# Two trunk layers on one core: index queries for 384 tokens, bias tables in tiles of their own, first x tiles on two queues

## The chip, the cores and the metric

The kernel runs on one core of one Trainium2 chip. The metric is device time in microseconds (us) of one execution, given as the median of three runs. A profiled execution has its own time; the span inside it runs from the first to the last instruction.

## What is computed

Two layers follow one another on 512 tokens of width 2048, in float32. Layer 0 (even) norms x, projects it and feeds two branches; the change is in the branch that picks keys:

```python
h = rms_norm(x, norm_g) @ w_in
p_in, p_gate, dq, dk, dv, d_gate, iq, ik, iw = split_cols(h, EVEN_SPLITS)
...
# per block of 128 queries, starting at token `start`:
s_idx = einsum('bqhe,bse->bqhs', iqb, ik) * IDX_DIM ** -0.5     # 16 index heads of 64
score = einsum('bqhs,bqh->bqs', relu(s_idx), iwb)
score = where(keys <= pos_q, score, -inf)
_, idx = top_k(score, 128)                                      # topk = 512 // 4
# attention over the chosen keys, with a T5 bias table
```

A query among the first 128 tokens has at most 128 keys, so the choice keeps all of them; the kernel computes index scores for the query blocks 1, 2 and 3 alone. Layer 1 (odd) is a sliding window attention with the same kind of bias table, and both layers end in an output projection and a residual sum.

## The kernel before

**Products.** Each float32 operand is held as two parts, a rounded one and the rest. One product of a 128x128 weight block is three matmuls, the helper `mm3` (lines 127 to 129). A projection is a job of 16 steps over the 2048 input channels in blocks of 128 (`col_job`): its step k multiplies weight block k by `acts[k]`, the transposed and split x of that block, with 512 tokens as moving columns. Jobs wait in a queue, and `pump(n)` emits n steps of it. `later(n, f)` calls f after n more steps.

**Weights.** `load_to` issues the loads of weight tiles `wr` on SyncE's (SP's) DMA queue; `split_to` has ScalarE (ACT) write the rounded part `wh` (line 101) and VectorE (DVE) the rest `wl` (line 107).

**The start.** Ahead of all jobs stands a loop over k = 0 to 15 that has its matmuls written out. Below, "tile k" is x's channel block k. `x_tile(k)` turns tile k by four transposes on TensorE (PE) into a PSUM bank of tag O (line 640), from which ACT writes the rounded part scaled by the norm gain (line 642), DVE the rest (line 643), and ACT (even k) or DVE (odd k) a copy (line 646) that SP stores to DRAM (line 647). Tag O has two banks, handed out in turn, and whoever takes a bank waits until its last content has been read. Step k of the loop holds: `mm3` on the first block of index queries, `x_tile(k + 2)`, the splits of coming weights, and twelve matmuls of 256 columns for keys, values and index keys (line 703, "the small group" below). Beside that ACT squares two pieces of x per step in the steps 3 to 10 (line 718). All engines work through their instructions in the order in which the program emits them.

**The first loads.** SP issues tile 0, two weight tiles, tile 1, then the first 512 channels of x (tiles 2 and 3 are read from these), a third weight tile and the next 512 channels. ACT issues the three gain vectors.

**Bias tables.** `bias_rows` (line 655) loads a one-hot table into a tile of tag `s2` (four buffers, which the copies of line 646 use too), emits a product with the bias table three steps later on PE, into a bank of tag O (line 661), and one step later a copy by ACT (line 665) and a store. It is called in steps 8, 9 and 10.

**After the loop** come seven jobs, of 16 steps each, for the other blocks of index queries. Among their steps stand `spread` (line 350, two banks of tag O), the key transposes and the index scores (line 974: 256, 384 and 512 columns). Then the choice of keys and all later work follow.

Of the kernel before, what the change touches and what calls it, by code (L numbers as in the profile page):

```python
# [10 lines left out]
F32 = mybir.dt.float32  # L11
# [3 lines left out]
OP = mybir.AluOpType  # L15
# [20 lines left out]
def trunk(ctx, tc, x, rel_bias, even_norm, even_w_in, even_pool_w, even_pool_scale, even_q_gain,  # L36
# [14 lines left out]
    def s2k():  # L51
        return sb.tile([P, 512], F32, tag="s2", name="s2", bufs=4)
# [73 lines left out]
    def mm3(o, wh, wl, xh, xl, start, stop):  # L126
        PE.matmul(o, wh, xh, start=start, stop=False)  # L127
        PE.matmul(o, wh, xl, start=False, stop=False)  # L128
        PE.matmul(o, wl, xh, start=False, stop=stop)  # L129
# [4 lines left out]

    def col_job(acts, w, ncols, c0, finish, hook=None):

        us = [plan_cols(w, ncols, c0, k0) for k0 in (0, 8)]

        def run():
            acc = bank("acc")  # L140
            for k in range(NK):
                u = us[k // 8] + k % 8 // 4
                hi, lo = view(u, 4)
                a = acts[k]
                flush(("split", id(a)))
                mm3(acc, hi[:, k % 4, :], lo[:, k % 4, :], a[:, 0, :], a[:, 1, :], k == 0, k == NK - 1)
                if k % 4 == 0:
                    split_to(u + 1 + AHEAD)
                if hook:
                    hook(k)  # L150
                if k == NK - 1:
                    finish(acc)
                yield
        queue.append(run())
        count["queued"] += NK
# [86 lines left out]

    def load_first(k):
        x_first[k] = s2k()
        nc.sync.dma_start(out=x_first[k].rearrange("p (i c) -> p i c", i=NT),
                          in_=ap(x2, k * P, [[D, P], [P * D, NT], [1, P]]))

    load_first(0)
    load_to(2)
    load_first(1)  # L250
    load_x(0)
    load_to(3)
    load_x(1)

# [8 lines left out]
    gain0, gain1, pscale = vecs[:, 0:16], vecs[:, 16:32], vecs[:, 32:40]  # L263
    vrow = sb.tile([P, 512], F32, tag="gt", name="vrow", bufs=2)[0:40, 0:P]
    qg0 = cst.tile([P, 1], F32, name="qg0")
# [4 lines left out]
    relb = cst.tile([33, 32], F32, name="relb")  # L270
    for r0, n, src in ((0, NK, even_norm), (16, NK, odd_norm), (32, 8, even_pool_scale)):
        nc.scalar.dma_start(out=vrow[r0:r0 + n], in_=ap(src, 0, [[P, n], [1, P]]))
# [381 lines left out]
    def bias_rows(oh, n0, n1, heads, dst):  # L654
        n = n1 - n0
        t = s2k()
        nc.sync.dma_start(out=t[0:33, :n], in_=oh[:, n0:n1])
# [22 lines left out]
    for j in range(1, 8):  # L680
        col_job(acts, w_in0, E_IN, IQ + j * P, lambda acc: stack(acc, P, 384, then=iq_st.append))
    split_to(1)
    vb = bank("O")
    PE.transpose(vb[:, 0:40], vrow, ident[0:40, 0:40])
    V.tensor_copy(out=vecs, in_=vb[:, 0:40])
    V.tensor_scalar(out=pscale, in0=pscale, scalar1=2.0, scalar2=None, op0=OP.mult)
    x_tile(0)
# [4 lines left out]
    for k in range(NK):  # L692
        sh, sl = view(s_half[k], 2)
        ih, il = view(q_half[k], 4)
        a = acts[k]
        mm3(iq_ps[0], ih[:, k % 4, :], il[:, k % 4, :], a[:, 0, :], a[:, 1, :], k == 0, k == NK - 1)
        if k + 2 < NK:
# [8 lines left out]
        if k == 1:  # L706
            load_x(2)
        if k == 3:
            load_x(3)
        if k == 6:  # L710
            load_constants()
        if k in (8, 9, 10):
            bias_rows(*((onehot0, 0, 512, 16, rv0), (onehot0, 512, 640, 16, rv0),
                        (onehot1, 0, 512, 32, rv1))[k - 8])
        if 3 <= k < 11:
# [187 lines left out]
    split_to(done["split"] + 4)  # L903
    stack(iq_ps[0], P, 384, then=iq_st.append)
    ssk = cst.tile([P, NT], F32, name="ssk")
# [323 lines left out]
```

## Time and profile before

| what | us |
|---|---|
| median of three runs | 1434.77 (1432.28 to 1435.99) |
| the profiled execution | 1435.47 |
| its span, first to last instruction | 1433.7 |
| TensorE busy in the span | 1414.7 |
| VectorE busy | 886.0 |
| ScalarE busy | 735.9 |

A row of the trace's timeline gives the start of an instruction or of a run of equal ones, its duration, its engine and line, what it writes and reads, and in brackets how long the engine had been idle and what released it. Matmuls overlap, so the rate of a stretch is read from the starts of its rows and not from their durations.

### The profile page before, as it was taken

To read this page: it belongs to the slowest core of one execution; us is meant where nothing else is said; L and a number is where in the kernel's file an instruction comes from. 1 tells how busy PE (TensorE), PEld (TensorE's weight loads), DVE (VectorE), ACT (ScalarE), POOL (GpSimd) and SP (SyncE) were. 2 spreads that over 40 slices of the span, in tenths; PEclk is the share of its full clock that TensorE was granted. 3 is DMA by queue.
4 is the path that set the end of the run, shared out by engine and by line. 5 is a ranking of instruction groups with operands and counts; after the bars stand their busy time and mean duration, and the time that the engine had idled before them with its cause. 6 is when DMAs were issued, how large, how long until landed. Compare 5 with 4: busy or idle time off the path is not lost.

```text
span 1433.7 us, 19902 instructions
## 1 busy us (share of the span) xinstructions
PE 1414.7 (99%) x7149; PEld 1180.3 (82%) x7149; DVE 886.0 (62%) x1663; ACT 735.9 (51%) x1641; POOL 331.7 (23%) x469
## 2 busy tenths in 40 slices
PE   7999999999999999999999999999999999999998
PEld 6788888888888888788888888788888888888887
DVE  4555679845687777733335468777777777753332
ACT  6544422323567676633335357666776757742221
POOL 1100001324546553111111143232232323100000
PEclk9999999999999999999999999999999999999999
DMA  9432333333432322265543232233232322334442
GB/s 286 139 88 74 89 103 89 96 102 96 114 82 86 103 74 74 74 173 144 147 139 103 86 113 85 71 96 100 80 101 85 96 86 84 100 118 154 129 158 74
DMA packets 228439, 153.84 MB, mean 107 GB/s; under 512 B 9001, under 2 KB 205698, under 8 KB 228340
## 3 DMA queue, kind: packets, MB, share of 16 engines
q1 hardware_dynamic: 228260, 152.55, 36.1%
q8 instruction: 56, 0.92, 0.3%
q14 instruction: 43, 0.35, 0.1%
q10 hardware_dynamic: 80, 0.02, 0.0%
HBM read 139.85 MB, written 12.69 MB: 106 GB/s over the span
## 4 chain that ended last, share of the span: by engine, by line
PE 91%; ACT 2%; DMA 2%; DVE 2%; issue 1%; SPq 1%; POOL 1%; DVEq 0%; ACTq 0%; POOLq 0%
PE ps_acc L127 21%; PE ps_acc L128 21%; PE ps_acc L129 21%; PE ps_S L171 5%; PE ps_T L171 5%; PE ps_O L523 3%; PE ps_S L459 3%; PE ps_acc L171 3%; PE ps_O L171 3%; PE ps_T L498 3%; PE ps_S L974 1%; DMA wr<-in_even_w_in 1%; DMA G<-rv 1%; DVE wl L107 1%; PE ps_O L855 0%
## 5 line engine op out<-in xcount | busy, mean ns | idle before, releaser
L107 DVE TENSOR_TENSOR wl<-wr,wh 128x512 fp32r<-128x512 f32 x440 | 332.7, 768 | 169.1 <-ACT wh L101 167.3
L101 ACT CAST wh<-wr 128x512 fp32r<-128x512 f32 x440 | 265.7, 617 | 225.6 <-PE ps_acc L128 89.0
L127 PE MATMUL ps_acc<-h,wh 128*128 128x512 f32 x640 | 254.5, 398 | 0.0
L128 PE MATMUL ps_acc<-h,wh 128*128 128x512 f32 x640 | 250.1, 391 | 0.0
L129 PE MATMUL ps_acc<-h,wl 128*128 128x512 f32 x640 | 250.1, 391 | 0.0
L127 PE MATMUL ps_acc<-h1s,wh 128*128 128x512 f32 x512 | 207.3, 405 | 0.0
L128 PE MATMUL ps_acc<-h1s,wh 128*128 128x512 f32 x512 | 200.7, 392 | 0.0
L129 PE MATMUL ps_acc<-h1s,wl 128*128 128x512 f32 x512 | 200.6, 392 | 0.0
L129 PEld LDWEIGHTS ps_acc<-h,wl 128*128 128x128 f32 x640 | 120.3, 188 | 26.4
L127 PEld LDWEIGHTS ps_acc<-h,wh 128*128 128x128 f32 x640 | 120.6, 188 | 22.4 <-issue 2.1
L128 PEld LDWEIGHTS ps_acc<-h,wh 128*128 128x128 f32 x640 | 120.8, 189 | 20.0
L478 ACT ACTIVATE L<-L,nmx 128x256 f32<-128x256 f32 (+1 forms) x192 | 99.8, 522 | 40.3 <-DVE nmx L473 32.3
L129 PEld LDWEIGHTS ps_acc<-h1s,wl 128*128 128x128 f32 x512 | 96.1, 188 | 21.6
L128 PEld LDWEIGHTS ps_acc<-h1s,wh 128*128 128x128 f32 x512 | 96.7, 189 | 13.8
L127 PEld LDWEIGHTS ps_acc<-h1s,wh 128*128 128x128 f32 x512 | 96.4, 188 | 14.0
L127 PE MATMUL ps_acc<-yh,wh 128*128 128x512 f32 x240 | 95.2, 397 | 0.0
L128 PE MATMUL ps_acc<-yh,wh 128*128 128x512 f32 x240 | 93.6, 390 | 0.5 <-DVE yh L414 0.5
L129 PE MATMUL ps_acc<-yh,wl 128*128 128x512 f32 x240 | 93.6, 390 | 0.0
L503 ACT CAST pt<-ps_T 128x512 fp32r<-128x512 f32 x104 | 57.1, 549 | 70.0 <-PE ps_T L498 70.0
L453 ACT ACTIVATE L<-L,rs 128x256 f32<-128x256 f32 (+1 forms) x192 | 85.2, 515 | 8.0 <-DVE rs L448 7.6
L504 DVE TENSOR_TENSOR pt<-ps_T,pt 128x512 fp32r<-128x512 f32 x104 | 66.8, 643 | 20.6 <-ACT pt L503 19.4
L459 PE MATMUL ps_S<-kT,qS 128*128 128x256 f32 (+2 forms) x384 | 72.8, 298 | 0.2 <-DVE L L463 0.2
(436 smaller groups left out, 2357.2 us busy)
## 6 DMA issues: line engine op xcount, KB each, us to landing
wr<-in_even_w_in SPq DMA_DIRECT2D x79, 512.0 KB, 3.8
wr<-in_odd_w_in SPq DMA_DIRECT2D x72, 512.0 KB, 3.9
wr<-in_even_w_out SPq DMA_DIRECT2D x32, 512.0 KB, 4.2
wr<-in_odd_w_out SPq DMA_DIRECT2D x32, 512.0 KB, 3.7
G<-rv SPq DMA_DIRECT2D x32, 192.0 KB, 4.3
xs<-in_x SPq DMA_DIRECT2D x16, 256.0 KB, 5.9
xT<-s SPq DMA_DIRECT2D x16, 256.0 KB, 4.3
G<-rv SPq DMA_DIRECT2D x16, 256.0 KB, 3.7
```

What stands on the lines that cost most here:

```text
L101: S.copy(hi, raw)
L107: V.tensor_tensor(out=lo, in0=raw, in1=rd(hi), op=OP.subtract)
L127: PE.matmul(o, wh, xh, start=start, stop=False)
L128: PE.matmul(o, wh, xl, start=False, stop=False)
L129: PE.matmul(o, wl, xh, start=False, stop=stop)
L171: PE.matmul(acc[i], a[:, xx, i * P:(i + 1) * P], u[ww][:, 0, :], start=(k == 0 and n == 0), stop=(k == NK - 1 and n == 2))
L453: S.activation(lb, lb, AF.Copy, scale=rs[:, b:b + 1])
L459: PE.matmul(s[:, dst:dst + kn], q[:, h, b * P:(b + 1) * P], kt()[:, part, k0:k0 + kn], start=part == 0, stop=part == 1)
L478: S.activation(lb, lb, AF.Exp, bias=nmx[:, b:b + 1], scale=1.0, accum_out=ss[:, b:b + 1])
L498: PE.transpose(tb[:, (2 * n + h) * P:(2 * n + h + 1) * P], self.L[h][:, u[1]:u[1] + P], ident)
L503: S.copy(hi[:, :w], tb[:, :w])
L504: V.tensor_tensor(out=lo[:, :w], in0=tb[:, :w], in1=rd(hi[:, :w]), op=OP.subtract)
```

## The change

The seven jobs and the first block multiply 384 tokens (128 to 511) where they multiplied 512; `stack` reads them from column 0. The first DMA of ACT is the gain vector of layer 0 alone, into a tile that is made earlier; the second is tile 1 of x, which leaves SP's queue. The first 512 channels of x are loaded in two halves, first the half with tiles 2 and 3. The gain vectors are turned in two steps: that of layer 0 ahead of tile 0, the others in step 1 of the loop. `bias_rows` takes tiles of tag `gt` (two buffers, which the gain rows and later the gates use) and is called in the steps 7, 8 and 13.

```diff
-    def col_job(acts, w, ncols, c0, finish, hook=None):
+    def col_job(acts, w, ncols, c0, finish, hook=None, t0=0):
...
-                mm3(acc, hi[:, k % 4, :], lo[:, k % 4, :], a[:, 0, :], a[:, 1, :], k == 0, k == NK - 1)
+                mm3(acc[:, :T - t0], hi[:, k % 4, :], lo[:, k % 4, :], a[:, 0, t0:], a[:, 1, t0:], k == 0, k == NK - 1)
...
-    load_first(0)
+    vrow = sb.tile([P, 512], F32, tag="gt", name="vrow", bufs=2)[0:40, 0:P]
+    nc.scalar.dma_start(out=vrow[0:NK], in_=ap(even_norm, 0, [[P, NK], [1, P]]))
+    load_first(0, nc.sync)
+    load_first(1, nc.scalar)
     load_to(2)
-    load_first(1)
-    load_x(0)
+    load_x(0, 256, 512)
     load_to(3)
+    load_x(0, 0, 256)
     load_x(1)
...
     def bias_rows(oh, n0, n1, heads, dst):
         n = n1 - n0
-        t = s2k()
+        t = sb.tile([P, 512], F32, tag="gt", name="oh", bufs=2)
...
-        col_job(acts, w_in0, E_IN, IQ + j * P, lambda acc: stack(acc, P, 384, then=iq_st.append))
+        col_job(acts, w_in0, E_IN, IQ + j * P, lambda acc: stack(acc, 0, 384, then=iq_st.append),
+                t0=P)
     split_to(1)
-    vb = bank("O")
-    PE.transpose(vb[:, 0:40], vrow, ident[0:40, 0:40])
-    V.tensor_copy(out=vecs, in_=vb[:, 0:40])
-    V.tensor_scalar(out=pscale, in0=pscale, scalar1=2.0, scalar2=None, op0=OP.mult)
+
+    def vectors(r0, r1):
+        vb = bank("O")
+        PE.transpose(vb[:, 0:r1], vrow[0:r1], ident[0:r1, 0:r1])
+        V.tensor_copy(out=vecs[:, r0:r1], in_=vb[:, r0:r1])
+
+    vectors(0, NK)
     x_tile(0)
...
-        mm3(iq_ps[0], ih[:, k % 4, :], il[:, k % 4, :], a[:, 0, :], a[:, 1, :], k == 0, k == NK - 1)
+        mm3(iq_ps[0][:, :384], ih[:, k % 4, :], il[:, k % 4, :], a[:, 0, P:], a[:, 1, P:], k == 0, k == NK - 1)
...
         if k == 1:
             load_x(2)
+            vectors(NK, 40)
+            V.tensor_scalar(out=pscale, in0=pscale, scalar1=2.0, scalar2=None, op0=OP.mult)
...
-        if k in (8, 9, 10):
-            bias_rows(*((onehot0, 0, 512, 16, rv0), (onehot0, 512, 640, 16, rv0),
-                        (onehot1, 0, 512, 32, rv1))[k - 8])
+        if k in (7, 8, 13):
+            bias_rows(*{7: (onehot0, 0, 512, 16, rv0), 8: (onehot0, 512, 640, 16, rv0),
+                        13: (onehot1, 0, 512, 32, rv1)}[k])
...
-    stack(iq_ps[0], P, 384, then=iq_st.append)
+    stack(iq_ps[0], 0, 384, then=iq_st.append)
```

SP's queue at its start, before (`s2` is a tile of x of its own, `wr` a weight tile, `xs` a piece of x with 128 tokens):

```order
L245 DMA s2_84<-in_x 128x4x128
L90 DMA wr_86<-in_even_w_in 128x2x128
L90 DMA wr_86<-in_even_w_in 128x2x80
...
L90 DMA wr_92<-in_even_w_in 128x4x128 x2
L245 DMA s2_95<-in_x 128x4x128
L220 DMA xs_68<-in_x 128x512
...
L90 DMA wr_101<-in_even_w_in 128x4x128
```

And in the changed kernel, the same place:

```order
L245 DMA s2_86<-in_x 128x4x128
L90 DMA wr_90<-in_even_w_in 128x2x128
L90 DMA wr_90<-in_even_w_in 128x2x80
...
L90 DMA wr_96<-in_even_w_in 128x4x128 x2
L220 DMA xs_68<-in_x 128x256
...
L90 DMA wr_103<-in_even_w_in 128x4x128
L90 DMA wr_103<-in_even_w_in 128x4x80
L220 DMA xs_68<-in_x 128x256
```

Tile 1 (`s2_95`) has left the queue for ACT's; ahead of the third weight tile stand half the columns of each piece of x, behind it the other half.

TensorE's queue from step 10 of the loop, before; the banks of tag O are written `ps_O` with a number: 580 is tile 12, 612 tile 13, 667 tile 14, 697 tile 15, and those of line 661 are bias products:

```order
L640 MATMUL ps_O_580<-ident_109,xs_80 128x128 [waits DMAHW4_49,PE_49,Activation_49]
...
L640 MATMUL ps_O_612<-ident_109,xs_80 128x128 [waits DVE_49,PE_49]
...
L661 MATMUL ps_O_637<-s2_529,relb_126 16x512 [waits DMAHW3_49,PE_49,DMAHW6_49,Activation_49,Pool_49]
...
L640 MATMUL ps_O_667<-ident_109,xs_80 128x128 [waits DVE_49,PE_49]
...
L661 MATMUL ps_O_689<-s2_571,relb_126 16x128 [waits DMAHW1_49,PE_49,Activation_49]
...
L640 MATMUL ps_O_697<-ident_109,xs_80 128x128 [waits Activation_49]
```

And in the changed kernel; 587 is tile 12, 619 tile 13, 676 tile 14, 704 tile 15, and line 663 is the bias product:

```order
L642 MATMUL ps_O_587<-ident_115,xs_80 128x128 [waits DMAHW0_49,PE_49,Activation_49]
...
L663 MATMUL ps_O_609<-oh_506,relb_131 16x512 [waits DMAHW1_49,DVE_49,DMAHW7_49,PE_49,Pool_49]
...
L642 MATMUL ps_O_619<-ident_115,xs_80 128x128 [waits PE_49,Activation_49]
...
L663 MATMUL ps_O_644<-oh_538,relb_131 16x128 [waits DMAHW3_49,Activation_49]
...
L642 MATMUL ps_O_676<-ident_115,xs_80 128x128 [waits DVE_49,PE_49]
...
L642 MATMUL ps_O_704<-ident_115,xs_80 128x128 [waits PE_49,Activation_49]
```

The first bias product has moved ahead of tile 13, so the two banks change hands in another order: tile 13 now follows tile 12 in its bank, the second product the first, and tile 15 the second product; each of these three waits names ACT, which empties the bank.

ScalarE's queue from tile 12's copy on, in the changed kernel (line 644 is the rounded part of a tile, 648 its copy, 726 a square, 667 the copy of a bias product; before, its line 665, all three copies of products stood behind tile 14's copy):

```order
L648 COPY s2_595<-ps_O_587 128x512
L726 ACTIVATE pt_612,ssq_p_188<-xs_82 128x512
L726 ACTIVATE pt_614,ssq_p_188<-xs_83 128x512
L644 ACTIVATE h_624<-ps_O_619,vecs_125 128x512
L101 CAST wh_629<-wr_356 128x512
L667 COPY oh_506<-ps_O_609 16x512
L644 ACTIVATE h_681<-ps_O_676,vecs_125 128x512
L648 COPY s2_684<-ps_O_676 128x512
L667 COPY oh_538<-ps_O_644 16x128
L644 ACTIVATE h_709<-ps_O_704,vecs_125 128x512
```

The first product's copy stands behind tile 13's rounded part, the second's behind tile 14's copy; the third has left this stretch, and its product stands behind step 1 of the first job.

## Rows read from the trace of the kernel before

**Rows 1.** The page: busy time, share of the span and instructions of each engine.

```profile
PE 1414.7 (99%) x7149; PEld 1180.3 (82%) x7149; DVE 886.0 (62%) x1663; ACT 735.9 (51%) x1641; POOL 331.7 (23%) x469
```

**Rows 2.** Waits of PE: waiter, waited for, us in total, times, longest.

```profile
PE ps_O L640 <- DMA s<-in_x: 3.5, 1, 3.5
PE ps_O L640 <- DVE s L646: 2.6, 1, 2.6
```

**Rows 3.** Stretches: length, busy us of each engine, granted clock, DMA share, GB/s.

```profile
10.00:15.00 5.00, 4.75 (x20) 3.92 (x19) 2.10 (x3) 1.89 (x3) 0.00 (x0) 1.00 1.08 349
...
45.00:50.00 5.00, 2.39 (x14) 1.91 (x14) 2.30 (x6) 1.99 (x5) 0.56 (x1) 0.93 0.37 124
50.00:55.00 5.00, 5.00 (x29) 4.13 (x28) 1.21 (x2) 2.24 (x5) 2.08 (x9) 0.73 0.58 171
...
60.50:160.00 99.50, 99.50 (x469) 83.60 (x468) 59.08 (x114) 47.63 (x103) 2.28 (x8) 1.00 0.30 82
```

**Rows 4.** Timeline of PE among the index jobs: start, us, line, operands, shape, count.

```profile
101.43 0.40 PE L127 MATMUL ps_acc<-h,wh 128*128 128x512 f32 x1
...
102.82 0.51 PE L974 MATMUL ps_S<-ikT,qS 128*128 128x384 f32 x2
103.17 0.40 PE L127 MATMUL ps_acc<-h,wh 128*128 128x512 f32 x1
...
104.55 0.61 PE L974 MATMUL ps_S<-ikT,qS 128*128 128x512 f32 x2
105.00 0.39 PE L127 MATMUL ps_acc<-h,wh 128*128 128x512 f32 x1
```

**Rows 5.** The page's group of weight loads for the third matmul of `mm3`.

```profile
L129 PEld LDWEIGHTS ps_acc<-h,wl 128*128 128x128 f32 x640 | 120.3, 188 | 26.4
```

**Rows 6.** Timeline of PE in the start.

```profile
9.21 1.09 PE L640 MATMUL ps_O<-ident,s 128*128 128x128 f32 x4 [3.55 <-DMA s<-in_x]
...
12.59 0.77 PE L703 MATMUL ps_S<-wh,h 128*128 128x256 f32 x2
...
44.09 1.01 PE L661 MATMUL ps_O<-s,relb 33*16 33x512 f32 x2 [0.53 <-issue]
...
48.61 0.63 PE L640 MATMUL ps_O<-ident,xs 128*128 128x128 f32 x4 [2.61 <-DVE s L646]
...
56.99 0.39 PE L703 MATMUL ps_S<-wh,h 128*128 128x256 f32 x2
...
58.41 0.40 PE L127 MATMUL ps_acc<-h,wh 128*128 128x512 f32 x1
...
60.53 0.40 PE L127 MATMUL ps_acc<-h,wh 128*128 128x512 f32 x1
...
64.64 1.05 PE L350 MATMUL ps_O<-ident,n0rh 128*128 128x128 f32 x8
```

**Rows 7.** Timeline of ACT in the start.

```profile
22.27 0.61 ACT L101 CAST wh<-wr 128x512 fp32r<-128x512 f32 x1
...
43.41 0.59 ACT L646 COPY s<-ps_O 128x512 f32<-128x512 f32 x1 [0.82 <-DVE h L643]
...
45.12 0.68 ACT L642 ACTIVATE h<-ps_O,vecs 128x512 fp32r<-128x512 f32 x1
45.69 0.61 ACT L101 CAST wh<-wr 128x512 fp32r<-128x512 f32 x1
49.27 0.69 ACT L642 ACTIVATE h<-ps_O,vecs 128x512 fp32r<-128x512 f32 x1 [2.97 <-PE ps_O L640]
...
51.27 0.57 ACT L665 COPY s<-ps_O 16x512 f32<-16x512 f32 x1
...
63.25 0.62 ACT L101 CAST wh<-wr 128x512 fp32r<-128x512 f32 x1 [1.97 <-PE ps_acc L128]
...
66.35 0.64 ACT L352 COPY n0R<-ps_O 128x512 f32<-128x512 f32 x1
```

**Rows 8.** Timeline of DVE: the copy of tile 13.

```profile
47.77 0.69 DVE L646 COPY s<-ps_O 128x512 f32<-128x512 f32 x1 [1.19 <-DMA xT<-s]
```

More of the change, by code (lines that the diff above doesn't have):

```diff
@@ L241, in trunk, with load_first @@
     x_first = {}
-    def load_first(k):
+    def load_first(k, queue):
         x_first[k] = s2k()
-        nc.sync.dma_start(out=x_first[k].rearrange("p (i c) -> p i c", i=NT),
+        queue.dma_start(out=x_first[k].rearrange("p (i c) -> p i c", i=NT),
                           in_=ap(x2, k * P, [[D, P], [P * D, NT], [1, P]]))
-    load_first(0)
+    vrow = sb.tile([P, 512], F32, tag="gt", name="vrow", bufs=2)[0:40, 0:P]
+    nc.scalar.dma_start(out=vrow[0:NK], in_=ap(even_norm, 0, [[P, NK], [1, P]]))
+    load_first(0, nc.sync)
+    load_first(1, nc.scalar)
     load_to(2)
-    load_first(1)
-    load_x(0)
+    load_x(0, 256, 512)
     load_to(3)
+    load_x(0, 0, 256)
     load_x(1)
@@ L263, in trunk @@
     gain0, gain1, pscale = vecs[:, 0:16], vecs[:, 16:32], vecs[:, 32:40]
-    vrow = sb.tile([P, 512], F32, tag="gt", name="vrow", bufs=2)[0:40, 0:P]
     qg0 = cst.tile([P, 1], F32, name="qg0")
@@ L270, in trunk @@
     relb = cst.tile([33, 32], F32, name="relb")
-    for r0, n, src in ((0, NK, even_norm), (16, NK, odd_norm), (32, 8, even_pool_scale)):
+    for r0, n, src in ((16, NK, odd_norm), (32, 8, even_pool_scale)):
         nc.scalar.dma_start(out=vrow[r0:r0 + n], in_=ap(src, 0, [[P, n], [1, P]]))
```

## The prediction

> **What bounds the kernel now.** I read the page's busy times first, then the waits of TensorE (PE), then stretches, then the timelines of the places that the change touches. PE is busy for 99% of the span, no other engine for more than 62% [rows 1], and the granted clock is 1.00 in the index jobs [rows 3]. So what is taken off PE's stream comes off the time, unless another engine becomes late in that stretch. All of PE's waits over 2 us on a thing that this change touches lie in the start, the first 60.5 us: 3.5 us for tile 1 of x and 2.6 us in front of tile 14 [rows 2].
>
> **Part one, the seven index jobs.** They hold 7 x 16 x 3 = 336 matmuls, now of 384 columns. Durations overlap, so I take starts. Between 101.43 and 102.82 lie six matmuls of 512 columns: 1.39 / 6 = 0.232 us each. Two of 384 columns take 102.82 to 103.17, 0.175 each; two of 512 columns of the same line take 104.55 to 105.00, 0.225 each [rows 4]. The difference is 0.057 across lines and 0.050 within line 974. I take 0.055, for in a job each matmul stands among equals as in the first pair: 336 x 0.055 = **18.5 us**, bounds 16.8 and 19.2.
>
> Cover in this stretch: of 99.5 us DVE is busy for 59.1 and ACT for 47.6 [rows 3]. With some 18.5 us gone these are 73% and 59% of it. DMA at a share of 0.30 goes to 0.37. None becomes the bound. The order of steps is the same, so the choice of keys, which DVE does behind it, begins as much earlier as PE does, and the gain is kept.
>
> **Part two, the beginning.** Before, PE waited 3.55 us for tile 1, whose load stood behind two weight tiles, and began the first small group at 12.59 [rows 6]. Now tile 1 is issued on ACT at once, and tiles 2 and 3 need half of the first x pieces: 0.52 MB less ahead of them, at the 349 GB/s of the stretch from 10 to 15 us [rows 3] 1.5 us. ACT's casts still stand ahead of the first index matmul, so tile 1's own 3.55 us are not won in full. I call the shift of the start s and take s = 1.5. Bounds: 0.5 (about one DMA issue of SP) and 2.5 (much of the wait for tile 1).
>
> The DMA share from 10 to 15 us is 1.08 [rows 3]: the engines have no room, so what shifts the start is the order of the bytes and not the second queue. The Trainium skill has this as a rule ("DMA: Bandwidth & Descriptors", section "Issuing engines are not separate DMA queues"): transfers started by several engines run on the same 16 DMA engines, and only issue time is saved. By that rule alone s would be near its lower bound, and the time 1 us later.
>
> **Part three, tiles 12 to 15 and the bias products.** In the loop's second half ACT is behind: from 22.27 to 45.12 [rows 7] it has squares, rounded parts, copies and casts, and it waits only for DVE inside a tile. Narrower matmuls cannot speed this up, so the 48 of the first block (48 x 0.055 = 2.6 us) get no term of their own. I carry ACT's times over less s.
>
> Before, three one-hot tables held three of the four `s2` buffers, tile 13's copy waited until the store of tile 12 landed (47.77) [rows 8], and tile 14 began at 48.61 after 2.61 us of idle PE [rows 6]. That wait goes. What is late next, by the order of the changed kernel's queues, is the bank of tag O:
> - Tile 13 follows tile 12 in its bank, whose copy by ACT ends at 43.41 + 0.59 = 44.00 [rows 7], less s. Its twelve small matmuls take 58.41 - 56.99 = 1.42 [rows 6], with the four transposes 1.8: to 45.8.
> - The second product needs the first one's copy, which ACT does behind tile 13's rounded part (45.12) and a cast (45.69, some 0.56 to the next) [rows 7]: 46.25 to 46.82. PE waits 1 us. Product 0.55, index matmuls 0.53: tile 14 at 47.9.
> - Tile 15 needs the second product's copy, behind tile 14's rounded part and copy. Before, from that rounded part's start to the copy of the (larger) product's start is 51.27 - 49.27 = 2.0 [rows 7]; so 47.9 + 0.65 + 2.0 + 0.25 = 50.8 to 50.9.
> - From there PE has four transposes, three small groups and two triples: 0.36 + 3 x 1.42 + 2 x 0.53 = 5.7.
>
> So the first job begins at 56.6 - s = 55.1, where it began at 60.53 [rows 6]: **5.4 us** gained. The first product may also wait for its table, but tile 13 behind it waits for ACT until 44.00 - s anyway, which covers a wait of a microsecond or two.
>
> In the 5.4 is a clock that does not fall. Before, the 2.6 us of idle were followed by a stretch at a granted 0.73 and one at 0.93, together 0.27 x 5 + 0.07 x 5 = 1.7 us [rows 3]. Now the idle is in pieces, the longest 1 to 1.6 us; the cost is between 0 and 1.7, and I take 0, since the pieces are nearer to the 0.53 us in front of 44.09 [rows 6] than to the 2.61. That same wait ended right behind ACT's copy of tile 12 at 44.00, so I take the bank and not the table as its cause, as I did for tile 13.
>
> **Part four, the third product.** It leaves the loop (that is in the 5.4) and now stands behind step 1 of the first job: two matmuls of 512 columns, 1.01 shown, 0.95 by the next start: **-0.95 us**. Its copy by ACT is emitted behind the casts for that job, the stacking of the first index queries, the squares of the keys and the values. Before, the last of the casts waits for PE and starts 63.25 - 60.53 = 2.7 after the job begins, and what follows ends where line 352 starts, 66.35, 3.1 later [rows 7]. Now the cast waits for eleven narrower matmuls and the product, 1.95 + 0.95 + 0.15 = 3.05; the copy ends at 3.05 + 3.1 + 0.57 = 6.7 after the job's begin. PE reaches the second bank of `spread` after six steps (3.15), the product and `spread`'s first bank (0.9): 5.0. This bank was the third product's. PE waits **-1.7 us**; bounds 0 (if the copy gets ahead) and 2.5. Whoever stands behind is all of PE's queue. The key transposes come 8 steps later and find their input ready.
>
> The gain vectors in two steps cost one small transpose and one copy in a start that waits for ACT: nothing, or 0.2 us if that cover is gone. The `gt` buffers have no other user in this stretch. The earlier placement of tables puts none of SP's weight loads behind a new long wait, since the stores before them wait for the same copies.
>
> **Sum.** 18.5 + 5.4 - 0.95 - 1.7 = 21.2 us (21.25). The profiled execution took 1435.47, 0.7 over the median: 1414.2 against its own time, 1434.77 - 21.2 = **1413.6** as a median. The lower bounds of the terms give 16.8 + (5.4 - 1.0 - 1.7) - 0.95 - 2.5 = 16.0, the upper 19.2 + 6.4 - 0.95 = 24.7: 1410 to 1419.
>
> **The rivals.**
> - The banks don't hold tiles 13 and 15 (ACT gets ahead when PE's idle goes). Then the start gains the 2.6 and 0.5 of idle, 1.7 of clock, s and the 2.6 of the first block, without the 1.7 of part four: 18.5 + 8.9 = 27.4, so 1407.4. For it speaks that ACT had idled for 2.97 us in front of tile 14 [rows 7]; against it that the waits stand in the order. 0.15.
> - The clock falls all the same, in the start or at the 1.7 us of `spread`: 1.7 to 2.5 less, so 1415.5. 0.2.
> - s is near its lower bound, and the sum's other terms hold: 1414.6 and up to 1416. 0.1.
> - The weight load sets the rate of the narrower matmul. Each has one of its own, 188 ns by the page [rows 5]: then 336 x (0.232 - 0.188) = 14.8, so 1417.3. Against it: twelve matmuls of 256 columns, each with a load of its own in the page's count, take 1.42 us, 0.118 each [rows 6]. 0.03.
> - Slower: the third product, on PE's queue behind step 1, waits for its one-hot table, whose DMA stands on SP's queue behind the store of tile 15. All of PE stands behind it, one us for each us that the table is late; the sum turns negative from 21 us on. The wait for tile 1, 3.5 us [rows 2], is far from that. 0.02.
>
> On the rate of narrower matmuls the Trainium skill ("TensorE: Matmul & The Clock Gate", section "Back-to-back issue gap") says that in a stream of load and matmul pairs both set the spacing, with 81 ns measured at 128 columns and 131 at 512. An estimate from these figures is 17 ns for 128 columns, 5.7 us for part one and a time of 1426.4. The trace disagrees with 0.057 and 0.050 us [rows 4], which is why I give that no more than the 0.03 of the rival above.
>
> **How the numbers follow.** The forecast, 1413.6, has 0.5. The range reaches from 1409, between the forecast's upper bound and the first rival, to 1417.5, over the clock, the small s and most of the weight load's case; left out are the first rival's centre and the slower case. A measurement can tell about 0.3% (4.3 us) from no change. Faster by more has 0.96, within 0.02, slower 0.02: only the last rival leaves the faster side.
>
> **What would show it.** In the changed trace the index matmuls start 0.175 apart; the first small group begins near 11; the wait of tile 13's copy for a store is gone; PE waits in front of tiles 13 and 15 and of the second product, for ACT; the first job begins near 55; PE waits some 1.7 us at `spread`'s second bank, for the copy of the third product. A first job that begins near 51.5 would make the first rival right, a granted clock under 1 around 45 us the second. The prediction is wrong in its main term if the index jobs' matmuls start 0.19 apart or more, or if DVE or ACT have PE waiting among the index scores.

## The result, and the profile after

The changed kernel takes **1416.4 us** (median of four runs, 1414.73 to 1419.48) where the kernel before takes 1435.1 beside it: a ratio of **0.9875**, 95% interval 0.9854 to 0.9897. The forecast was 1413.6, the range 1409.0 to 1417.5. So the time lies inside the range, 2.8 us above the point. The profiled execution took 1416.52 with a span of 1414.7, 19.0 us less than the span before.

Three marks on PE's timeline split that span: the first matmul of the first index job, the last matmul of the index scores, and the end.

| us | start, to the first job | jobs, to the last index score | rest of the span |
|---|---|---|---|
| before | 60.53 | 107.58 | 1265.59 |
| after | 56.35 | 94.25 | 1264.10 |
| gained | 4.2 | 13.3 | 1.5 |
| forecast | 5.4 | 15.85 | 0 |

The forecast of the jobs is the 18.5 of part one less the 0.95 and 1.7 of part four. Both stretches that the change touches gave less than forecast (1.2 and 2.5), and the rest gave 1.5 that the change does not explain.

The page's busy times of after: PE is still the bound, with 18.0 us less work than in [rows 1].

```profile
PE 1396.7 (99%) x7150; PEld 1176.5 (83%) x7150; DVE 885.0 (63%) x1664; ACT 734.8 (52%) x1641; POOL 330.9 (23%) x469
```

Timeline of PE among the index jobs of after (start, us, line, operands, shape, count), as [rows 4]: six matmuls of 384 columns from 98.12 to 99.17 and six from 99.51 to 100.55, so 0.175 and 0.173 us each, where the same two places before, from 101.43 and from 103.17, had 0.232 and 0.230.

```profile
98.12 0.34 PE L127 MATMUL ps_acc<-h,wh 128*128 128x384 f32 x1
...
99.17 0.51 PE L982 MATMUL ps_S<-ikT,qS 128*128 128x384 f32 x2
99.51 0.33 PE L127 MATMUL ps_acc<-h,wh 128*128 128x384 f32 x1
...
100.55 0.63 PE L982 MATMUL ps_S<-ikT,qS 128*128 128x512 f32 x2
```

Timeline of PE in the start of after, as [rows 6]; the bracket is the idle time in front and what ended it:

```profile
5.36 1.09 PE L642 MATMUL ps_O<-ident,s 128*128 128x128 f32 x4 [0.48 <-DMA s<-in_x]
9.62 0.69 PE L127 MATMUL ps_acc<-h,wh 128*128 128x384 f32 x1 [3.18 <-ACT wh L101]
...
11.62 0.78 PE L709 MATMUL ps_S<-wh,h 128*128 128x256 f32 x2
...
17.68 0.33 PE L642 MATMUL ps_O<-ident,xs 128*128 128x128 f32 x1 [0.31 <-DMA xs<-in_x]
18.32 0.33 PE L642 MATMUL ps_O<-ident,xs 128*128 128x128 f32 x1 [0.31 <-DMA xs<-in_x]
...
40.97 1.01 PE L663 MATMUL ps_O<-oh,relb 33*16 33x512 f32 x2 [1.03 <-DVE wl L107]
...
43.26 0.99 PE L642 MATMUL ps_O<-ident,xs 128*128 128x128 f32 x4 [0.55 <-ACT s L648]
...
50.52 0.66 PE L642 MATMUL ps_O<-ident,xs 128*128 128x128 f32 x4 [0.24 <-ACT s L648]
...
56.35 0.34 PE L127 MATMUL ps_acc<-h,wh 128*128 128x384 f32 x1
...
63.33 0.39 PE L356 MATMUL ps_O<-n0rstd,flip 128*128 128x4 f32 x2 [1.63 <-ACT oh L667]
```

Tile 1 is turned at 5.36 where it was at 9.21, but the wait has only changed its owner. Tile 1's 3.55 us for a DMA [rows 2] have become 3.18 for ACT's cast, and the first small group begins at 11.62 where it began at 12.59. Then tile 4, line 642 at 17.68 and 18.32, waits for its piece of x, which it had not done. Further on the bank waits stand where the prediction put them: ACT's copy in front of tiles 13 (0.55) and 15 (0.24), and 1.63 at `spread`'s second bank. The wait that was forecast in front of the second product does not show in after, where the matmuls ahead of it run at a lower clock (below); it is 0.70 in e7. The wait of 2.61 for the store is gone.

Stretches of after (length, busy us of PE, PEld, DVE, ACT and POOL, granted clock, DMA share, GB/s), as [rows 3]:

```profile
42.50:45.00 2.50, 1.95 (x11) 1.74 (x10) 0.09 (x1) 2.38 (x7) 0.00 (x0) 0.69 0.95 288
45.00:47.50 2.50, 2.50 (x13) 2.05 (x13) 2.19 (x5) 0.98 (x3) 0.14 (x1) 0.63 0.20 63
...
62.50:65.00 2.50, 1.67 (x7) 1.67 (x8) 2.50 (x12) 1.26 (x4) 2.03 (x6) 0.78 0.15 33
65.00:67.50 2.50, 2.50 (x10) 2.50 (x10) 2.46 (x13) 0.62 (x1) 0.24 (x2) 0.54 0.00 0
```

The clock fell twice, each time right behind idle of PE: behind the 1.03 and 0.55 us near 41 and 43, and behind the 1.63 at 63.33. In between it is at 1.00. In each fall the granted clock is at half, the lower level of 1.2 GHz, for some three us (0.50 from 64.5 to 67.0): the matmuls of 384 columns from 64.08 to 67.28 start 0.32 apart.

Timeline of ACT in after, as [rows 7]: the copy of tile 12, the rounded part of tile 14, and the copy of the third product.

```profile
42.62 0.58 ACT L648 COPY s<-ps_O 128x512 f32<-128x512 f32 x1 [0.82 <-DVE h L645]
...
48.37 0.69 ACT L644 ACTIVATE h<-ps_O,vecs 128x512 fp32r<-128x512 f32 x1 [2.38 <-PE ps_O L642]
...
62.72 0.56 ACT L667 COPY oh<-ps_O 32x512 f32<-32x512 f32 x1
```

The copy of tile 12 starts 0.79 us earlier than in [rows 7]. That is the shift s, at the very place on which the prediction's chain was built, and it was forecast as 1.5.

### The profile page after: what moved, and what is told of

It is laid out like the page before. It is cut to its first block, busy times and chain, and to the rows that moved or that the text cites. A ratio compares the mean times of both kernels' runs of the same rounds, so it can differ in the third digit from the quotient of the medians.

```text
span 1414.7 us, 19908 instructions
## 1 busy us (share of the span) xinstructions
PE 1396.7 (99%) x7150; PEld 1176.5 (83%) x7150; DVE 885.0 (63%) x1664; ACT 734.8 (52%) x1641; POOL 330.9 (23%) x469
## 4 chain that ended last, share of the span: by engine, by line
PE 93%; ACT 2%; DMA 2%; DVE 1%; issue 1%; POOL 0%; SPq 0%; ACTq 0%; DVEq 0%
PE ps_acc L127 21%; PE ps_acc L128 21%; PE ps_acc L129 21%; PE ps_S L171 5%; PE ps_T L171 5%; PE ps_S L461 3%; PE ps_O L525 3%; PE ps_acc L171 3%; PE ps_O L171 3%; PE ps_T L500 3%; PE ps_S L982 1%; PE ps_O L863 0%; PE ps_T L567 0%; ACT wh L101 0%; ACT pt L726 0%
## 5 line engine op out<-in xcount | busy, mean ns | idle before, releaser
L127 PE MATMUL ps_acc<-h,wh 128*128 128x512 f32 (+1 forms) x640 | 247.6, 387 | 3.2 <-ACT wh L101 3.2
L129 PE MATMUL ps_acc<-h,wl 128*128 128x512 f32 (+1 forms) x640 | 243.9, 381 | 0.0
L128 PE MATMUL ps_acc<-h,wh 128*128 128x512 f32 (+1 forms) x640 | 243.7, 381 | 0.0
```

## The experiments

**The theory at the start.** The columns carry nearly all of the gain. The start gains some four us and gives most of it back at the third product. The 2.8 us to the forecast are a smaller s and the two falls of the clock. **The rival:** the start (buffers and loads) gives several us of its own, and the columns less than 17.

All kernels in one table, from their timelines and times. The shift is read from the copy of tile 12 by ACT; ratios are to the kernel before, beside which each ran (its medians there were 1434.8 to 1436.3, so times of different groups of runs compare by their ratios).

| kernel | copy of tile 12 | start | jobs | rest | time, us | ratio, 95% |
|---|---|---|---|---|---|---|
| before | 43.41 | 60.53 | 107.58 | 1265.6 | 1435.1 | 1 |
| before, once more (e12) | 43.64 | 60.95 | 107.58 | 1265.2 | 1435.46 | |
| after | 42.62 | 56.35 | 94.25 | 1264.1 | 1416.4 | 0.9875 (0.9854 to 0.9897) |
| after, once more (e10) | 43.35 | 57.08 | 94.27 | 1265.1 | 1415.65 | 0.9864 (0.985 to 0.9878) |
| e1, columns only | 41.50 | 59.92 | 89.94 | 1265.6 | 1416.57 | 0.9859 (0.9841 to 0.9877) |
| e2, all but the columns | 43.42 | 56.92 | 110.28 | 1264.6 | 1434.36 | 0.9993 (0.9985 to 1.0002) |
| e7, loads as before | 42.85 | 55.84 | 92.66 | 1265.2 | 1415.0 | 0.986 (0.9844 to 0.9876) |
| e5, other order of x | 42.45 | 55.44 | 93.00 | 1265.3 | 1415.65 | 0.9866 (0.9847 to 0.9884) |
| e3, third product late | 42.81 | 55.80 | 91.80 | 1266.8 | 1415.28 | 0.9856 (0.9841 to 0.987) |
| e4, all products late | 42.50 | 52.23 | 96.71 | 1265.4 | 1416.59 | 0.9867 (0.9853 to 0.9882) |
| e8, late, tables early | 42.80 | 52.52 | 93.90 | 1265.8 | 1413.64 | 0.9856 (0.9834 to 0.9878) |
| e9, e8 and e5 | 42.70 | 52.43 | 94.38 | 1264.9 | 1413.36 | 0.9848 (0.9829 to 0.9867) |
| e11, e8, old start | 42.23 | 51.95 | 93.96 | 1265.1 | 1414.33 | 0.9848 (0.9835 to 0.9862) |

The stretches come from one profiled execution each. How far that carries is shown by the two executions each of before and of after: the jobs agree to 0.02 us, the start and the copy differ by 0.2 to 0.7, the rest by 0.4 and 0.9.

### Which part carries the gain: e1 and e2

e1 is the kernel before with the columns alone (the new argument `t0` and the columns of `stack` go with it, as in the change):

```diff
-                mm3(acc, hi[:, k % 4, :], lo[:, k % 4, :], a[:, 0, :], a[:, 1, :], k == 0, k == NK - 1)
+                mm3(acc[:, :T - t0], hi[:, k % 4, :], lo[:, k % 4, :], a[:, 0, t0:], a[:, 1, t0:], k == 0, k == NK - 1)
...
-        mm3(iq_ps[0], ih[:, k % 4, :], il[:, k % 4, :], a[:, 0, :], a[:, 1, :], k == 0, k == NK - 1)
+        mm3(iq_ps[0][:, :384], ih[:, k % 4, :], il[:, k % 4, :], a[:, 0, P:], a[:, 1, P:], k == 0, k == NK - 1)
```

> The kernel before with the narrower index matmuls alone; the start keeps its loads, its bias tiles and their steps. Theory (the narrower columns are nearly the whole gain, the changed start gives back at the start of the index jobs what it wins in the loop): the first index job begins at 60 to 60.5, since ScalarE and the store of tile 12 set the loop and not the width; the index jobs are 336 x 0.0545 = 18.3 us shorter, so 1416 to 1417.5, level with the changed kernel. Rival (the changed start is worth the 4 us that the first job begins earlier): 1420 to 1421.

e2 is the changed kernel with the columns put back to 512 at these lines.

> The changed kernel with index matmuls of 512 columns again. Theory: the first job begins near 56.8, the wait at the second bank of spread is shorter (6 steps take 1 us more, the third product's copy is no later), and the time is 1434 to 1436, no gain that can be measured. Rival: 1431, the 4 us of the earlier first job kept.

Measured: e1 1416.57, level with the changed kernel; e2 1434.36, level with the kernel before (ratio 0.9993, interval 0.9985 to 1.0002). **The columns are the gain; the rest of the change has none that can be measured when it stands alone.**

The table shows why. e1's jobs are 107.58 - 89.94 = 17.6 us shorter: that is part one by itself, with no product among the jobs and no wait but 0.4 us at the key transposes. In its start the copy of tile 12 comes 1.9 us earlier than before, yet the first job begins only 0.6 earlier, since PE then waits longer. Timelines of PE in e1 (the first product, tile 14, the second product) and of ACT (the copy of tile 14, which waits for the store of an earlier tile):

```profile
42.19 1.01 PE L661 MATMUL ps_O<-s,relb 33*16 33x512 f32 x2 [0.75 <-issue]
...
45.42 0.63 PE L640 MATMUL ps_O<-ident,xs 128*128 128x128 f32 x4 [1.50 <-DVE s L646]
...
50.54 0.60 PE L661 MATMUL ps_O<-s,relb 33*16 33x128 f32 x2 [3.06 <-ACT s L646]
```

```profile
49.91 0.58 ACT L646 COPY s<-ps_O 128x512 f32<-128x512 f32 x1 [3.12 <-DMA xT<-s]
```

0.75, 1.50 and 3.06 are 5.31 us of waits, where the start before had 0.53 and 2.61 [rows 6]. The 3.06 is for the store: what is faster ahead of a late store waits longer for it. The 1.50 is for DVE's copy of tile 13, which waited for no store in e1; it followed ACT's rounded part of that tile. In e2 the first job begins 3.6 us earlier than before, and the jobs take 2.7 longer: the third product (57.71, 1.04 us) and a wait of 1.26 at `spread`'s second bank now stand among them.

### What the new first loads are worth: e7, e5, e12 and e11

e7 is the changed kernel with the first loads as before:

```diff
-    load_first(1, nc.scalar)
     load_to(2)
-    load_x(0, 256, 512)
+    load_first(1, nc.sync)
+    load_x(0)
     load_to(3)
-    load_x(0, 0, 256)
     load_x(1)
```

> The changed kernel with its first loads of x as the kernel before has them: all on SP, the second weight tile ahead of tile 1, the first piece whole. The gain vectors stay ahead of them. Theory: this takes the 0.8 us of earlier start away and nothing else. PE waits 3 to 3.6 us for tile 1, the first job begins at 57.0 to 57.4 and the time is 1417.0 to 1417.5. Rival, the prediction's own s of 1.5 us: 57.9 and 1417.9. Second rival, nothing in the loop depends on it because ACT's copies set the pace: 56.4 and level with the changed kernel.

e5 is the changed kernel with tile 4's piece of x ahead:

```diff
     load_to(3)
-    load_x(0, 0, 256)
     load_x(1)
+    load_x(0, 0, 256)
```

> The changed kernel with one thing turned round: the piece of x that holds channels 512 to 1023, which tile 4 needs, is asked for ahead of the second half of the first piece. Theory: the start moved by only 0.8 us because tile 4 waited twice for that piece (0.31 and 0.31 us at 17.7 and 18.3). Then both waits go, the first index job begins at 55.7 to 55.9 where it began at 56.35, and the time is 1415.6 to 1416.0 where the changed kernel had 1416.4. Rival: ACT sets the loop's second half alone, so PE's earlier tile 4 only waits later: tile 4's waits go, but the first job still begins within 0.2 us of 56.35 and the time is level.

e12 is the kernel before once more, for a second profile.

> The kernel before once more, unaltered, for a second profile of its start. In the first, the small matmuls of 256 columns stood 0.21 us apart until 16.6 us and 0.12 from there; in other kernels' profiles that step came anywhere between 12.8 and 16.1. Theory: its place is a matter of the execution, not of the kernel; then it may stand elsewhere here, and with it the copy of tile 12 moves by up to 1 us from 43.41. Rival: it belongs to the order of the loads; then it stands at 16.6 again and the copy at 43.4. Tile 14's wait for the store (2.6 us) is there in both cases.

Measured: e7 takes 1415.0 and e5 1415.65, both level with the changed kernel. In e7 PE waits again in front of tile 1, for 4.86 us (3 to 3.6 were expected; the row names DVE as the last that came), and the first small group begins at 12.66 (11.62 in after), but the copy of tile 12 starts at 42.85 (42.62 and 43.35 in after). The second rival of e7's expectation holds: nothing behind depends on the new loads. (The first jobs of e7 and e5, at 55.84 and 55.44, are earlier than any of their expectations, which were reckoned from after's 56.35 with its fall of the clock; see e10.) In e5 tile 4's two waits are gone, and the copy of tile 12 comes at 42.45, beside 42.50 in e4 and 42.81 in e3, which have the loads of after. So the copy stands at 43.41, 43.64 and, in e2 with the new loads, 43.42 with 512 columns, and at 42.45 to 43.35 with 384 columns and the changed kernel's two-step vectors. **As far as the profiles tell, what there is of the shift s goes with the narrower first block and not with the loads.**

Where s is settled can be read exactly: at the fifth index triple of the loop. Timelines of PE, this triple in before and in after:

```profile
22.91 0.40 PE L127 MATMUL ps_acc<-h,wh 128*128 128x512 f32 x1
```

```profile
22.31 0.34 PE L127 MATMUL ps_acc<-h,wh 128*128 128x384 f32 x1
```

From its start to the copy of tile 12 pass 20.30 or 20.31 us in all ten profiles with 384 columns and 20.48 to 20.50 in the three with 512. So from there on the pace is the same in all of these kernels, as the prediction had it for ACT, and the narrower matmuls give nothing more than the 0.18 of this one triple. What they give lies ahead of it: four triples narrowed, 12 x 0.055 = 0.66 us. The triple starts at 22.91, 23.15 (e12) and, with the new loads, 22.94 (e2) with 512 columns; with 384 it starts at 21.20 (e1), 21.92 (e11) and 22.55 (e7) with the old loads and at 22.14 to 23.04 in the seven profiles with the new ones. The new loads do not bring it forward in either group. Since one kernel's two profiles differ by up to 0.73 (22.31, and 23.04 in e10), this is the likeliest reading of thirteen profiles and not shown by any pair of them.

Two reasons why the earlier tile 1 is worth nothing can be read. First, ACT's own chain begins later when tile 1's load runs beside that of the first weights (DMA share 1.09 from 2.5 to 5 us, 0.92 before). Timelines of ACT: its first cast in the kernel before, and in after.

```profile
5.17 0.62 ACT L101 CAST wh<-wr 128x512 fp32r<-128x512 f32 x1 [1.27 <-DMA wr<-in_even_w_in]
```

```profile
5.93 0.62 ACT L101 CAST wh<-wr 128x512 fp32r<-128x512 f32 x1 [1.48 <-DMA wr<-in_even_w_in]
```

0.76 us later (5.1 to 5.5 in the five profiles with the old loads, 5.8 to 6.2 in the eight with the new ones), and the first index triple stands behind the casts that follow (the 3.18 at 9.62): it starts only 0.33 earlier than before. Second, tile 4's piece of x is late by the new order: its four transposes take in after from 16.95 to 18.41, 1.46 us, where tile 5's take 0.35.

What is left is blurred by something else: the small matmuls of the first groups run at half their pace up to some point. Timeline of PE in e8, whose start is that of after:

```profile
13.60 0.63 PE L709 MATMUL ps_T<-wh,h 128*128 128x256 f32 x2
14.03 0.41 PE L709 MATMUL ps_T<-wl,h 128*128 128x256 f32 x1
...
16.18 0.40 PE L709 MATMUL ps_S<-wh,h 128*128 128x256 f32 x2
16.42 0.28 PE L709 MATMUL ps_S<-wl,h 128*128 128x256 f32 x1
```

Two of them take 0.43 us to the next start at 13.60 and 0.24 at 16.18. Read from small matmuls and index triples together, the change to full pace came at 12.8 us in after, 13.6 in e10, 14.0 in e4, 14.5 in e3 and 15.4 in e8, which all have the same start. So its place differs between executions. e12 adds nothing to that: it stands at 15.2 and 15.1 in the two profiles of before. The 16.6 of its expectation was only the next small group, for the triple ahead of it, from 15.24, already ran at full pace, 0.23 apart. In e1, which is at full pace from 12.9 on, this change explains, as an estimate, some 1.1 us (half of the 2.3 us from 12.9 to 15.2) of the 1.9 by which its copy of tile 12 is earlier than before's.

e11 has the whole start of the kernel before, its loads and the gain vectors in one step (their first DMA behind the others' again), with the 384 columns and e8's late products (below):

```diff
-    load_first(1, nc.scalar)
     load_to(2)
-    load_x(0, 256, 512)
+    load_first(1, nc.sync)
+    load_x(0)
     load_to(3)
-    load_x(0, 0, 256)
     load_x(1)
...
-    vectors(0, NK)
+    vectors(0, 40)
...
-            vectors(NK, 40)
```

> e8_late_tables_early with the whole start of the kernel before: its first loads in their old order on SP, and the gain vectors loaded behind them and transposed in one step. Left of the change are the 384 columns and the one-hot tables in buffers of their own. Theory: the new start gives nothing. Its earlier tile 1 is lost at tile 4, whose piece of x lands late, and at the second transpose of gain vectors (0.4 us of PE), while the narrower first block gives its 0.6 us in either. Then the fifth index triple of the loop starts at 21.2 to 22.2 where e8 has 22.49, the copy of tile 12 at 41.5 to 42.6 where e8 has 42.80, and the time is 0 to 1.3 us under e8's 1413.64: 1412.3 to 1413.6. Rival, the prediction's step: the new loads move the start earlier by 1 us and more; then this kernel's triple starts later than 22.5 and it takes 1414.5 or more.

Measured: the fifth triple at 21.92 (e8 22.49), the copy of tile 12 at 42.23 (e8 42.80), the first job at 51.95 (e8 52.52), the time 1414.33 against e8's 1413.64, level (ratios 0.9848 and 0.9856). The triple and the copy came as the theory had them; the time lies between the theory's 1413.6 and the rival's 1414.5. So the old start is worth no less than the new one. The second transpose of gain vectors can be seen at work: in e7 1.79 us lie between the small group at 15.81 and the triple at 17.60 that follows this transpose, where e1 takes 1.51 (14.90 to 16.41). It was priced at nothing or 0.2, and is 0.3 here. Its effect on the time is too small to be measured.

### The falls of the clock: e10

e10 is the changed kernel unaltered.

> The changed kernel once more, unaltered, with a profile of its own. Theory: the two stretches of lower granted clock in its first profile (0.69 and 0.63 from 42.5 to 47.5 us, 0.78 and 0.54 from 62.5 to 67.5) belong to that execution and not to the order of the work, since e7_loads_as_before has waits of the same lengths at the same places and a clock of 1.00 throughout. Without them the first index job begins at 55.5 to 55.8 and the last index score at 148.2 to 148.5, 2.1 to 2.4 us earlier than in the first profile, and such an execution takes 1414 to 1415. Rival: the falls are this kernel's own; then they stand at the same places again, the first job begins near 56.3 and the last score near 150.6.

Stretches of e10 and, below, of e7, whose waits are as long (1.07 and 0.51 near 41 and 43, 1.63 at 62.83):

```profile
45.00:47.50 2.50, 2.50 (x13) 2.23 (x12) 1.73 (x3) 1.71 (x5) 0.00 (x0) 0.50 0.28 98
...
65.00:67.50 2.50, 2.50 (x9) 2.50 (x9) 2.47 (x15) 0.62 (x1) 0.79 (x5) 0.50 0.06 14
```

```profile
45.00:47.50 2.50, 1.80 (x13) 1.34 (x13) 2.19 (x5) 1.22 (x3) 0.00 (x0) 1.00 0.10 25
...
65.00:67.50 2.50, 2.50 (x17) 2.47 (x16) 2.10 (x9) 0.00 (x0) 0.00 (x0) 1.00 0.00 0
```

The falls stood there again, so the expectation that they would be gone failed for this execution (its first job came at 57.08, later than the rival's 56.3 too, by as much as its copy of tile 12). They are not in every execution of this kernel either: the mean granted clocks of the four runs that were timed first were 0.998, 0.996, 0.998 and 1.000, with 1416.52, 1419.48, 1416.29 and 1414.73 us. Three lost some clock, one did not and was the fastest. Of e10's four runs the profiled one had 0.998 and took 1418.24, the other three 0.999 to 1.000 and 1415.38 to 1415.83. And e7, e5 and e3, with waits of much the same length at 41 to 46 us, had 1.00 there.

What a pair of falls costs can be read well, since the work around it is alike. From the copy of tile 12 to the first job: 13.73 us in both profiles of after, 12.99 in e7, e5 and e3. That is 0.74. The jobs: 94.25 and 94.27 against e7's 92.66, with the same wait of 1.63 within: 1.6. Together **2.3 us**. What decides in a given execution whether the clock falls at these waits is left open.

### The third product and the other two: e3, e4, e8 and e9

e3 moves the third product behind the key transposes, 20 steps after its call:

```diff
-                        13: (onehot1, 0, 512, 32, rv1)}[k])
+                        13: (onehot1, 0, 512, 32, rv1, 20)}[k])
...
-        later(3, product)
+        later(wait, product)
```

> The changed kernel with the third bias product 17 steps later, behind spread and the key transposes. Theory (PE waits at spread's second bank for the copy of the third product, and the clock falls for that wait): the wait of 1.6 us is gone, the granted clock from 60 to 70 us is 1.00 (0.83 in the changed kernel), 3 to 4 us faster than the changed kernel, 1412.5 to 1413.5. Rival (the wait moves on to the key transposes, whose input ScalarE and VectorE make): level with the changed kernel, 1416, with an idle PE at the key transposes.

Measured: the wait at `spread` is gone, the clock stays at 1.00 from 40 to 80, and the last index score starts at 147.60 where after has 150.60. That is the 3.0 expected up to there, but not all of it is the moved product: 0.55 lies ahead of the first job, where the edit touches nothing, and against e7, whose clock did not fall either, the jobs are only 0.86 shorter (91.80, 92.66). The time is 1415.28, some 1 us under the changed kernel and not outside its spread, since the profile lost 2.7 us again in the rest (1266.8 against 1264.1). There a fall of the clock (0.34 x 5 = 1.7 us) stands behind a wait of 2.18 us in layer 1 (1.3 in after), in a stretch that the edit does not touch. Stretches of e3:

```profile
890.00:895.00 5.00, 2.82 (x25) 1.94 (x24) 3.16 (x7) 1.69 (x6) 0.00 (x0) 1.00 0.22 77
895.00:900.00 5.00, 5.00 (x20) 4.15 (x21) 3.77 (x9) 2.99 (x9) 2.41 (x4) 0.66 0.36 105
```

e4 moves all three products behind the key transposes, each table loaded 3 steps ahead of its product:

```diff
-        if k in (7, 8, 13):
-            bias_rows(*{7: (onehot0, 0, 512, 16, rv0), 8: (onehot0, 512, 640, 16, rv0),
-                        13: (onehot1, 0, 512, 32, rv1)}[k])
...
+    bias_rows(onehot0, 0, 512, 16, rv0)
+    bias_rows(onehot0, 512, 640, 16, rv0)
     pump(4)
     for j in range(8):
+        if j == 2:
+            bias_rows(onehot1, 0, 512, 32, rv1)
```

> The changed kernel with all three bias products behind the key transposes. Theory (in the loop the bias products make tiles 13 and 15 and the second product wait for ScalarE): no wait of PE for ScalarE's copies from tile 12 on, granted clock 1.00 from 40 to 50 us, the first job at 52.5 to 53.5 instead of 56.35 (1.5 of it only moved, since 1.5 us of products stand later), and the 3 to 4 us of the third product as well: 1410 to 1411.5. Rival (ScalarE's squares set the loop anyway): first job at 55, 1412.5.

Measured: the first job begins at 52.23, 4.1 us earlier than in after and near the 51.5 that the prediction's first rival had put for the changed kernel: without products in the loop no bank holds tiles 13 and 15. But the time is 1416.59, level. Timeline of PE and stretches of e4:

```profile
67.64 1.45 PE L663 MATMUL ps_O<-oh,relb 33*16 33x512 f32 x4 [1.40 <-DVE wl L107]
```

```profile
65.00:70.00 5.00, 3.60 (x15) 2.23 (x14) 2.04 (x5) 2.23 (x5) 0.00 (x0) 0.85 0.39 116
70.00:75.00 5.00, 5.00 (x26) 4.96 (x25) 2.48 (x4) 1.38 (x3) 0.00 (x0) 0.81 0.41 113
```

The first late product waited for 1.40 us, and behind it the clock lost (0.15 + 0.19) x 5 = 1.7. The line names DVE as the one that came last, but DVE's parts are of no use to this product; the table's landing was the guess. e8 tests it: the first two tables are loaded in the loop, where the changed kernel loads them, 30 and 34 steps ahead of their products, the third 14 steps ahead.

```diff
         if k in (7, 8):
-            bias_rows(*{7: (onehot0, 0, 512, 16, rv0), 8: (onehot0, 512, 640, 16, rv0)}[k])
+            bias_rows(*{7: (onehot0, 0, 512, 16, rv0, 30), 8: (onehot0, 512, 640, 16, rv0, 34)}[k])
...
+        if j == 2:
+            bias_rows(onehot1, 0, 512, 32, rv1, 14)
```

> The changed kernel with all three bias products behind the key transposes, as in e4_all_late, but with the first two one-hot tables loaded in the loop, at the steps at which the changed kernel loads them, and the third 14 steps ahead of its product. Theory: e4's wait of 1.40 us in front of its first late product was the table's landing, and the clock's fall behind it (0.85 and 0.81 from 65 to 75 us, some 1.7 us) was that wait's consequence. Then the first index job begins at 52.2 as in e4, no wait stands in front of a product, the granted clock is 1.00 from 60 to 80, the last index score starts at 145.5 to 146 where e4 had 148.94, and the time is 1411.5 to 1413.5. Rival: the clock falls elsewhere, behind the key transposes' wait of 0.56 us or in layer 1 near 895 as in e3_third_late, and gives 2 to 3 us back: 1414 to 1416.

> e8_late_tables_early and e5_x_order in one kernel. If the start is set by the landing of x, the first index job begins 0.5 to 0.7 us ahead of e8's, near 51.6, and the time is that much under e8's, 1411 to 1413. If ACT sets the loop, it is level with e8 (within 0.3 us at the first job).

Measured: in e8 no product waits and the clock is 1.00 from 60 to 80, so the wait was the table's and the loss behind it went with it. The first job begins at 52.52, the last score stands at 146.42 (expected 145.5 to 146), the time is 1413.64, at the upper end of the expectation. e9 takes 1413.36 with its first job at 52.43, so e5's order of x adds nothing here either. e9's runs (1412.71 to 1413.91) and e11's (1412.78 to 1414.48) all lie below those of both samples of the changed kernel (1414.73 to 1419.48 and 1415.38 to 1418.24). e11 ran beside e10. So the products behind the key transposes, with tables loaded early, are faster than both kernels, by 1 to 3 us over the changed one; e8's own runs (1412.64 to 1417.93) overlap with it, and so do the intervals of the ratios.

Of the 3.8 us by which e8's first job is earlier than after's, its jobs hand back a part (93.90, where e7 has 92.66). All three products stand among them now (0.96, 0.32 and some 0.95 by the next starts), and the key transposes come so early that they wait for their input:

```profile
60.96 0.60 PE L955 MATMUL ps_O<-ident,kdt 128*128 128x128 f32 x4
...
62.01 1.48 PE L955 MATMUL ps_O<-ident,kdt 128*128 128x128 f32 x4 [0.45 <-DVE kdt L945]
```

In e3 it is the same: from 64.24, where they start, to the next matmul at 66.09 they take 1.85 us, where they take 0.79 in after. DVE's key rows are the next wait of this stretch.

## Why the prediction was right, and what was off, point by point

- **Part one, 18.5.** Right in mechanism and nearly in size. The spacing is 0.173 to 0.175 as said; over the whole stretch e1 shows 17.6, or 0.0525 for each of 336, between the two pairs of [rows 4]. Off by 0.9, of which 0.4 is another thing: e1 comes to the key transposes earlier and takes 1.19 us for them, where before took 0.79. The rival that the weight load sets the rate is out.
- **No cover becomes the bound.** Right: among the jobs of after PE waits at one place only, that of part four.
- **Part two, s = 1.5.** The step that was mis-sized, and its reason was wrong. s was 0.8 in the profile, 0.06 in e10's, 0.6 to 1.0 in e3 to e9. It was argued from the bytes ahead of tiles 2 and 3; e7 shows that these are worth nothing at the end of the loop, and in e2, without the narrower first block, to which the prediction had given no term, s is 0. The reason for that missing term, that ACT is behind, holds only from the fifth triple on; the four triples ahead of it and this one are 15 x 0.055 = 0.8 us. The small-s rival came closest here, with another mechanism than its own.
- **Part three, the first job at 56.6 - s.** Right. In the three profiles with no fall of the clock the shifts are 0.56 (e7), 0.96 (e5) and 0.60 (e3), so 56.04, 55.64 and 56.00 by the sum; measured 55.84, 55.44 and 55.80, 0.2 less each time. The banks hold tiles 13 and 15 and the second product as written out (0.51, 0.24 and 0.70 in e7). The banks' rival is out; e4 and e8 show what it would have taken, the products out of the loop, and that most of its gain is then spent among the jobs. The 0.53 in front of the first product, in the kernel before, had been put down to tile 12's bank, and that is borne out: the product began 0.09 after the end of that copy in before and in e12, and 0.11 in e1. In the changed kernel it has another bank, and its idle of 1.03 is another wait. There the product began at 40.97, ahead of tile 12's copy at 42.62, and in e5 and e10 the same place names the one-hot table's DMA (timeline of PE in e5):

```profile
41.26 1.01 PE L663 MATMUL ps_O<-oh,relb 33*16 33x512 f32 x2 [1.49 <-DMA oh<-in_onehot]
```

  So there it waits for its table, as e4's first product did. The prediction had covered that, for tile 13 waits behind it anyway.
- **A clock that does not fall, 0.** Wrong for the profiled execution, by 2.3 us, and the rival with 0.2 is what happened: 1415.5 was its time, 1416.4 was measured. It named both places and a price of 1.7 to 2.5.
- **Part four, -0.95 and -1.7.** Right: the wait at `spread` is 1.63, and e7's jobs are 92.66 - 89.94 = 2.72 us longer than e1's, where 2.65 was the sum.
- **The third product late enough to turn the sign.** Out: its table had landed.

In the profile's own time the forecast of 21.25 becomes 18.95 measured: -0.7 for s, -2.3 for the clock, -0.9 for part one, +0.2 in part three, -0.1 in part four and +1.5 in the rest. That last is no work of the change: the rest is 1264.1 to 1266.8 in all of these kernels, and after's is the least of them. So a part of the nearness is luck: without the 1.5 this execution would have gained 17.5 us, close to the slow end of the range.

## What to carry to other kernels

Price a narrower operand on the engine that sets the end by the distance of starts among equals: that was 93% of the result here (17.6 of 18.95 us), and it could be read from two pairs of rows. Give an earlier load nothing until the chain behind it has been followed to the first place where another engine is late anyway; here the wait only passed from a DMA to ACT. And when work is moved off one queue's stall, look for the next wait in the place where it lands, its inputs' landing included: the third product, and e4's first, lost there much of what the start had gained.

## What the runs showed of the hardware

- Idle of PE of 1 to 2 us was followed by some three us of half the granted clock in both profiles of after, and by none in e7, e5 and e3 at waits of the same length. Behind the longer idle of 2.61 (before), 2.73 (e12) and 3.06 us (e1) it fell each time. The pair of falls cost 2.3 us, more than the longer of the waits that they followed.
- In every start the first small matmuls ran at half the later pace (0.43 us for two against 0.24), up to a point between 12.8 and 15.4 us that differed between executions of the same kernel, in stretches whose granted clock is shown as 1.00. The spacing, 0.21 each, is the one that they have in after from 44.48 to 46.40, where the granted clock is 0.50. The rows do not show what this is.
